# Spreading a two-way state-space scan between the q, k, v projections and the gate

## The chip, the cores and the metric

The kernel runs on one core of a Trainium2 chip. The metric is device time in microseconds of one execution, as the median of several runs. The engines of the core are TensorE (PE, with PEld for its weight loads), VectorE (DVE), ScalarE (ACT), GpSimd (POOL) and SyncE (SP); each works through its instructions in order, and they wait for each other through semaphores. SP and ACT also issue DMAs, each from its own in-order queue.

## The reference

One block of a hybrid encoder, 1024 tokens of 1024 channels in float32. The parts that the change touches are the state-space mixer and the q, k, v projections beside it:

```python
h = rmsnorm(x, norm_mix_w)
z, xbc, dt_raw, q, k, v = jnp.split(h @ w_in, offs, axis=-1)
# ssd_mixer, per direction, in chunks of 128 tokens, 16 heads of 64 in 2 groups, state 128:
a_cum = jnp.cumsum(ac, axis=2)
decay = jnp.exp(jnp.where(lower, a_cum[:, :, :, None] - a_cum[:, :, None, :], -jnp.inf))
cb = jnp.einsum("bclgn,bcsgn->bclsg", cc, bc)
y_diag = jnp.einsum("bclsge,bcsgep->bclgep", cb[..., None] * decay, xc)
chunk_states = jnp.einsum("bclgn,bclgep->bcgepn", bc, xc * decay_to_end[..., None])
_, h_in = lax.scan(lambda h, i: (i[1][..., None, None] * h + i[0], h), h0, (chunk_states, chunk_decay))
y_off = jnp.einsum("bclgn,bcgepn->bclgep", cc, h_in) * jnp.exp(a_cum)[..., None]
# y = forward + backward + d_skip * x, then
g = y * silu(z); g = g * rsqrt(mean(g * g) + eps) * norm_w     # per group of 512 channels
```

Behind it stand neighbourhood attention on q, k, v, an output projection over both halves, and a squared-ReLU MLP.

## The kernel before, in words

Every large product is made of three float32r matmuls: an operand is split into a rounded part (`hi`, a ScalarE copy) and a rest (`lo`, a subtraction on DVE or POOL), and `mm3` (L179-182) adds hi x hi, hi x lo and lo x hi in PSUM. A piece of a projection is 8 x 3 such matmuls, 128 rows by 512 columns.

The order of the program is: x, its norm and transposes; the convolution channels (px) and the decays; the gate z in 2 x 8 pieces (pz, SiLU into `zs` at L497, stored to sz_dr); then the scan together with the q, k, v projections; then attention with the output projection as filler; then the MLP. Weights of a projection come in four tiles of 512 KB (`wraw`, loaded on SP) that ScalarE and DVE split (`wh`, L150; `wl`, L151).

The scan and the projections are written one behind the other, and the framework's scheduler weaves them: it sets each engine's order from its own estimate of times. The scan is the loop over `i` and `g` that calls `backward(7 - i, g)` and `forward(i, g)`: 16 turns, in each a chunk of the backward and one of the forward direction. `backward` loads x (`xs`), multiplies C by B (`pcb`, L575), and makes the two-way decay block of eight heads in two halves: a 512 KB broadcast load of the running sums into `rb` (L593), two POOL subtractions (L600), a predicated copy on DVE that takes one direction below the diagonal and the other above (L606), the exponent on ScalarE (L611), the product with pcb on DVE (L613) and eight matmuls `pd` (L618; each is two halves in the trace). `carried` (py, L555) adds what the state of a direction brings into a chunk; `decay_state` (pS) moves the state on: it splits the weighed x (L528, L529), adds into `st` (L538) and splits the state (L541, L542). A partial sum of a chunk goes to y1_dr (the trace's y_dr) until the other direction comes by; `gated` (L562 to L567) multiplies with the gate, norms and stores to y_dr. pcb, py and pS share two PSUM buffers (`ps_s`).

`qkv_proj` makes 48 pieces (pq): q, k and v in eight pieces each, for each of two groups of heads, in three PSUM buffers. `normed_split` (L683 to L693 and the split after it) norms each q and k piece, transposes it (ptq) right behind it, splits it and stores it from the ScalarE queue.

The pools of the scan (`qs`) take the memory that the convolution's and gate's pool (`qp`) gave back, so the first scan tile waits for the last gate piece; the attention's pools take that of `qs`.

Of the kernel before, what the change touches and what calls it, by code (L numbers as in the profile page):

```python
# [56 lines left out]
def hymba_block(  # L57
# [66 lines left out]
    y1_dr = dr.tile([NT, P, D], F32, name="y1_dr")  # L124
# [54 lines left out]
    def mm3(pt, ah, al, bh, bl, first, last):  # L179
        nc.tensor.matmul(pt, lhsT=ah, rhs=bh, start=first, stop=False)  # L180
        nc.tensor.matmul(pt, lhsT=ah, rhs=bl, start=False, stop=False)  # L181
        return nc.tensor.matmul(pt, lhsT=al, rhs=bh, start=False, stop=last)  # L182

# [24 lines left out]
    with ExitStack() as ph:  # L208
# [21 lines left out]
        with ExitStack() as p0:  # L230
# [14 lines left out]
            for h in range(2):  # L245
# [31 lines left out]
                dg = rp.tile([P, 4, P], F32, tag="dg", name="dg")  # L277
# [29 lines left out]

        def proj_col(get, m, h, pt):
# [4 lines left out]

        with p1:
            qp = p1.enter_context(tc.tile_pool(name="qp", bufs=2, side="right", reuse_waits="tile"))
# [168 lines left out]


# [3 lines left out]
            for g in range(2):  # L489
                get = load_w_nat(w_in[0], 0, KD, OFF_Z + 512 * g, nc.vector)  # L490
                for t in range(NT):
                    pt = ps_mm("pz")
                    for k in range(KD):
                        s = (slice(None), k, slice(t * P, (t + 1) * P))
                        mm3(pt, hTh[s], hTl[s], *get(k), k == 0, k == KD - 1)
                    zs = qp.tile([P, 512], F32, tag="zs", name="zs")
                    nc.scalar.activation(zs, pt, AF.Silu, scale=rcol[:, t : t + 1])  # L497
                    nc.scalar.dma_start(szb[:, t, :, g * 512 : (g + 1) * 512], zs)

        def hb(v):  # L500
            return v.unsqueeze(2).broadcast_to([P, 8, HD])

        def h8(v):
            return v.rearrange("p (e d) -> p e d", d=HD)

        with ExitStack() as p2:
# [14 lines left out]
            st = [[None, None], [None, None]]  # L521

            def decay_state(d, c, g, xw):
                prev = st[d][g]
                pS = ps_s("pS")
                xh = qp.tile([P, 512], F32R, tag="xh", name="xh", bufs=1)
                xl = qp.tile([P, 512], F32R, tag="xl", name="xl", bufs=1)
                nc.scalar.activation(xh, xw, AF.Copy)  # L528
                nc.vector.tensor_tensor(xl, xw, xh.bitcast(F32), op=sub)  # L529
                mm3(pS, bNh[:, c, g, :], bNl[:, c, g, :], xh, xl, True, True)  # L530
                new = prev and prev[0]
                if prev is None:
                    new = qp.tile([P, 512], F32, tag=f"st{d}{g}", name="st", bufs=1)
                    nc.vector.tensor_copy(new, pS)
                else:
                    dec = ed[:, d, c, 8 * g : 8 * g + 8]
                    nc.gpsimd.tensor_tensor(h8(new), h8(new), hb(dec), op=mul)
                    nc.vector.tensor_tensor(new, new, pS, op=add)  # L538
# [182 lines left out]

# [680 lines left out]
```

## Time and profile before

| | us |
|---|---|
| median of 3 runs | 1671.18 (1670.56 to 1671.56) |
| the profiled execution | 1675.21 |
| its span, first to last instruction | 1673.4 |
| PE busy in the span | 1594.3 (95%) |
| DVE busy | 1027.3 (61%) |
| ACT busy | 722.5 (43%) |
| POOL busy | 721.8 (43%) |

A matmul's busy time runs until its end, and the next one starts before that, so a busy TensorE need not be at its pace: what counts is the time from start to start. The granted clock is 1.00 at full speed; a mean below that in a stretch means that part of it ran at half clock. A tile's number is left out in the names, so `y` is y1 and `c` is c1.

### The profile page before, as it was taken

Reading aid. Unit: us, or ns where it says so; the run is one execution under the profiler, and the core shown is the slowest. Engines: PE = TensorE matmul, PEld = TensorE weight load, DVE = VectorE, ACT = ScalarE, POOL = GpSimd, SP = SyncE. Lnnn points to the kernel's source line nnn. Section 1 sums busy time; section 2 is a strip of 40 time slices with the busy share of each in tenths; the row PEclk is TensorE's granted clock in tenths of the full one; section 3 lists DMA queues with packets and bytes.
Section 4 is the critical chain, followed back from the end, with each engine's and each line's share of the span. In section 5 each row is a group of like instructions: output and inputs, shape, how many; then the busy total and the mean of one; then the engine's idle time right before and its main releaser. Section 6 shows DMA issues by size and latency. Waiting matters only on the chain. (4 is left out here: it accounts for less than half of the span.)

```text
span 1673.4 us, 20880 instructions
## 1 busy us (share of the span) xinstructions
PE 1594.3 (95%) x7462; PEld 1296.9 (78%) x7462; DVE 1027.3 (61%) x1432; ACT 722.5 (43%) x1195; POOL 721.8 (43%) x520
## 2 busy tenths in 40 slices
PE   7999999899998899999999989999999979999999
PEld 6788888777776677887887777788888868888887
DVE  4777214889796852666675567434243388887863
ACT  5434223434343442566665433554444444433330
POOL 3000004788688762233334232344444465455551
PEclk9999999999999999999999999999999999999999
DMA  8113337776666884987674240343354386644331
GB/s 206 52 38 114 87 99 226 208 193 195 223 216 185 225 266 176 279 212 204 174 208 133 89 164 38 138 164 131 133 166 149 129 295 230 219 145 151 101 101 76
DMA packets 181026, 273.49 MB, mean 163 GB/s; under 512 B 14691, under 2 KB 105915, under 8 KB 180923
## 3 DMA queue, kind: packets, MB, share of 16 engines
q1 hardware_dynamic: 136939, 231.26, 45.3%
q10 hardware_dynamic: 42976, 37.23, 7.3%
q0 software_dynamic: 1008, 3.67, 0.5%
q8 instruction: 59, 0.97, 0.2%
q14 instruction: 44, 0.36, 0.1%
HBM read 188.88 MB, written 86.56 MB: 165 GB/s over the span
## 5 line engine op out<-in xcount | busy, mean ns | idle before, releaser
L748 POOL TENSOR_TENSOR wl<-wraw,wh 128x1024 fp32r<-128x1024 f32 x110 | 298.8, 2728 | 318.4 <-ACT wh L747 305.1
L747 ACT ACTIVATE wh<-wraw 128x1024 fp32r<-128x1024 f32 x110 | 115.5, 1054 | 151.3 <-PE px L733 51.3
L733 PE MATMUL px<-wh,ahl 128*128 128x512 f32 x512 | 160.9, 391 | 4.6 <-ACT ahl L747 3.3
L180 PE MATMUL pq<-wh,hTh 128*128 128x512 f32 x384 | 152.7, 400 | 4.8 <-ACT wh L150 4.8
L181 PE MATMUL pq<-wl,hTh 128*128 128x512 f32 x384 | 152.3, 398 | 5.2 <-DVE wl L151 5.2
L733 PE MATMUL px<-h,wh 128*128 128x512 f32 x496 | 155.8, 394 | 1.4 <-DVE x L1089 1.4
L182 PE MATMUL pq<-wh,hTl 128*128 128x512 f32 x384 | 152.0, 397 | 0.0
L748 DVE TENSOR_TENSOR ahl<-ar,ahl 128x1024 fp32r<-128x1024 f32 x56 | 114.8, 2058 | 23.2 <-ACT ahl L747 22.1
L747 ACT ACTIVATE ahl<-ar 128x1024 fp32r<-128x1024 f32 x56 | 58.2, 1052 | 140.0 <-PE px L733 76.3
L733 PEld LDWEIGHTS px<-wh,ahl 128*128 128x128 f32 x512 | 96.1, 188 | 26.0 <-ACT ahl L747 3.7
L733 PEld LDWEIGHTS px<-h,wh 128*128 128x128 f32 x496 | 92.8, 187 | 24.4 <-ACT h L186 1.6
L151 DVE TENSOR_TENSOR wl<-wraw,wh 128x1024 fp32r<-128x1024 f32 x40 | 54.7, 1373 | 82.5 <-ACT wh L150 81.9
L733 PE MATMUL px<-wl,ahl 128*128 128x512 f32 x256 | 99.9, 390 | 0.0
L733 PE MATMUL px<-h,wl 128*128 128x512 f32 x248 | 97.8, 394 | 0.0
L181 PEld LDWEIGHTS pq<-wl,hTh 128*128 128x128 f32 x384 | 72.9, 190 | 22.2 <-DVE wl L151 8.0
L180 PEld LDWEIGHTS pq<-wh,hTh 128*128 128x128 f32 x384 | 72.8, 190 | 21.5 <-ACT wh L150 7.1
L186 ACT ACTIVATE pth<-ptp 128x384 fp32r<-128x384 f32 (+1 forms) x128 | 56.8, 456 | 67.1 <-PE ptp L947 66.6
L600 POOL TENSOR_TENSOR rb<-rb,c 128x512 f32<-128x512 f32 x64 | 76.1, 1210 | 20.3 <-DMA rb<-cum_dr 17.4
L182 PEld LDWEIGHTS pq<-wh,hTl 128*128 128x128 f32 x384 | 72.9, 190 | 14.7
L150 ACT ACTIVATE wh<-wraw 128x1024 fp32r<-128x1024 f32 x58 | 61.0, 1057 | 53.1 <-PE px L181 24.1
L733 PE MATMUL pz<-h,wh 128*128 128x512 f32 x256 | 81.9, 400 | 0.7 <-DVE h L187 0.7
L733 PE MATMUL pz<-wh,ahl 128*128 128x512 f32 x256 | 80.5, 391 | 0.0
(271 smaller groups left out, 4081.2 us busy)
## 6 DMA issues: line engine op xcount, KB each, us to landing
ar<-act_dr SPq DMA_DIRECT2D x56, 512.0 KB, 3.6
act_dr<-cq SPq DMA_DIRECT2D x49, 512.0 KB, 3.0
wraw<-in_w_in_dram SPq DMA_DIRECT2D x44, 512.0 KB, 4.3
rb<-cum_dr SPq DMA_DIRECT2D x32, 512.0 KB, 6.7
wraw<-in_w_mlp_in_dram SPq DMA_DIRECT2D x32, 512.0 KB, 4.6
wraw<-in_w_mlp_out_dram SPq DMA_DIRECT2D x32, 512.0 KB, 4.2
q_dr<-hl ACTq DMA_DIRECT2D x64, 128.0 KB, 3.0
k_dr<-hl ACTq DMA_DIRECT2D x16, 512.0 KB, 4.4
```

The source lines that it names most:

```text
L150: nc.scalar.activation(hi[:, 0:n], raw[:, 0:n], AF.Copy)
L151: lo_eng.tensor_tensor(lo[:, 0:n], raw[:, 0:n], hi[:, 0:n].bitcast(F32), op=sub)
L180: nc.tensor.matmul(pt, lhsT=ah, rhs=bh, start=first, stop=False)
L181: nc.tensor.matmul(pt, lhsT=ah, rhs=bl, start=False, stop=False)
L182: return nc.tensor.matmul(pt, lhsT=al, rhs=bh, start=False, stop=last)
L186: top = nc.scalar.activation(hi, src, AF.Copy)
L600: nc.gpsimd.tensor_tensor(rb[:, d], rb[:, d], c1[:, d, c, h0 : h0 + 4].unsqueeze(2).broadcast_to([P, 4, P]), op=sub,)
L733: nc.tensor.matmul(pt, lhsT=a, rhs=b, start=f, stop=l, skip_group_check=True)
L747: nc.scalar.activation(hl[0], src, AF.Copy)
L748: eng.tensor_tensor(hl[1], src, hl[0].bitcast(F32), op=sub)
```

## The change

Nothing is computed otherwise; the order and the place of the scan's steps change.

- The backward states are made beside the gate (`beside`, called behind each of the 16 gate pieces and the first five q pieces): x is loaded at piece n, weighed and split at n + 2, multiplied at n + 4, and each state is stored to sb_dr for later.
- Twenty of the 32 half blocks of decays, before the exponent, are made there too, and stored to seg_dr; the other twelve in the scan's first steps. All these stores are issued on ScalarE, behind a piece's SiLU or square.
- The scan is 16 steps, group 0 first and then group 1, with chunks 0 to 7 in each; a step makes both directions of its chunk. `prepare` loads x, the finished blocks (`gm`), the backward state (`sb`) and takes the exponent; `carry`, `inside` and `carried` follow one piece of q, k, v, `carried` of the forward direction the next, and `finish` (pd, gate, store) the one after. `issue_after(mark)` keeps a step's matmuls behind the last matmul of that piece. Steps 1, 3, ... 13 have a further piece behind them.
- The transposes of a q or k piece stand behind the next piece.
- The sums y1_dr are gone, C is split once per chunk, and pcb takes its PSUM from the transposes' two buffers.

The diff, with the removed `decay_state`, `carried`, `backward`, `forward` and the two projection loops left out:

```diff
+        def normed(pt, rt):
+            qn = hp.tile([P, 512], F32, tag="qn", name="qn", bufs=2)
+            act = nc.scalar.activation(qn, pt, AF.Square, scale=rt)
...
+        def qkv_units():
+            held = None
+            for g in range(2):
+                for off in (OFF_Q, OFF_K, OFF_V):
+                    for b, pt, rt, mark in qkv_proj(off, g):
+                        if held is not None:
+                            held(mark)
+                            held = None
...
+                            qn, act = normed(pt, rt)
+                            held = partial(store_q if off == OFF_Q else store_k, g, b, qn)
+                        yield mark, act
...
+        def seg_make(rb, g, c, q):
+            h0 = 8 * g + 4 * q
+            for d in range(2):
+                nc.gpsimd.tensor_tensor(
+                    rb[:, d],
+                    rb[:, d],
+                    c1[:, d, c, h0 : h0 + 4].unsqueeze(2).broadcast_to([P, 4, P]),
+                    op=sub,
+                )
+            nc.vector.copy_predicated(
+                rb[:, 0], lmask.unsqueeze(1).broadcast_to([P, 4, P]), rb[:, 1]
+            )
+
+        def seg_store(rb, g, c, q):
+            nc.scalar.dma_start(seg_dr[g, c, :, q], rb[:, 0].rearrange("p h s -> p (h s)"))
...
+            pq.close()
+            zp = p1.enter_context(tc.tile_pool(name="zp", bufs=2, side="right", reuse_waits="tile"))
...
+            def beside(n, mark, act):
+                with tc.issue_after(act):
+                    while st_:
+                        c, g, new = st_.pop(0)
+                        nc.scalar.dma_start(sb_dr[g, c - 1], new)
+                    while made:
+                        seg_store(*made.pop(0))
+                if n - 4 in hl_:
+                    c, g = back[n - 4]
+                    hl = hl_.pop(n - 4)
+                    pS = ps_s("pS")
+                    with tc.issue_after(mark):
+                        mm3(pS, bNh[:, c, g, :], bNl[:, c, g, :], *hl, True, True)
...
+                if n - 2 in xs_:
+                    c, g = back[n - 2]
+                    hl_[n - 2] = weighed(zp, 3, 1, c, g, xs_.pop(n - 2))
+                for m in rb_.pop(n - 2, ()):
+                    made.append(m)
+                    seg_make(*m)
+                if n < 14:
+                    c, g = back[n]
+                    xs_[n] = zp.tile([P, 512], F32, tag="xs", name="xs", bufs=3)
+                    nc.sync.dma_start(xs_[n], xs_dr[c, :, g * 512 : (g + 1) * 512])
+                if 0 < n < 18:
+                    rb_[n] = []
+                    for _ in range(2 if n in (5, 9, 13) else 1):
+                        sg = segs.pop(0)
+                        rb_[n].append((seg_load(zp, 4, *sg), *sg))
...
+                    beside(8 * g + t, mark.ins, act.ins)
+            units = qkv_units()
+            for n in range(16, 21):
+                beside(n, *next(units))
...
+            for n, (c, g) in enumerate(steps):
+                xs, gms, chl, shl, xhl = held
+                if xhl:
+                    carry(c, g, xhl, mark)
+                y1 = inside(c, g, xs, gms)
+                if shl:
+                    carried(1, c, g, chl, shl, y1, mark)
+                while made:
+                    seg_store(*made.pop(0))
+                mark, _ = next(units)
                 if c > 0:
+                    carried(0, c, g, chl, ahead[g], y1, mark)
+                if xhl:
+                    ahead[g] = split_state(g)
+                if n + 1 < len(steps):
+                    held = prepare(*steps[n + 1])
+                if segs:
+                    sg = segs.pop(0)
+                    made.append((seg_load(qp, 1, *sg), *sg))
+                    seg_make(*made[-1])
+                mark, _ = next(units)
+                finish(c, g, xs, gms, y1, mark)
+                if n % 2 and n < 14:
+                    mark, _ = next(units)
+            for _ in units:
+                pass
```

How the order moves on TensorE. Before, in the middle of the q pieces (pq is a piece's product, pd the block's, pS and py the state's):

```order
L182 MATMUL pq<-wh,hTl 128x512
L618 MATMUL pd<-xs,rb 128x64 x4
L180 MATMUL pS<-xh,bNh 128x512
L181 MATMUL pS<-xl,bNh 128x512
L182 MATMUL pS<-xh,bNl 128x512
L618 MATMUL pd<-xs,rb 128x64 x4
L180 MATMUL py<-sh,ch 128x512
L181 MATMUL py<-sl,ch 128x512
L182 MATMUL py<-sh,cl 128x512
L693 MATMUL ptq<-ident,qn 128x128 x4
L180 MATMUL pq<-wh,hTh 128x512
```

After, among the v pieces, where one piece of 24 ends and the next begins (mm3 stands at L181 to L183 there):

```order
L183 MATMUL pq<-wh,hTl 128x512
L181 MATMUL pS<-xhl,bNh 128x512
L182 MATMUL pS<-xhl,bNh 128x512
L183 MATMUL pS<-xhl,bNl 128x512
L705 MATMUL pcb<-cT,bT 128x128
L181 MATMUL py<-shl,chl 128x512
L182 MATMUL py<-shl,chl 128x512
L183 MATMUL py<-shl,chl 128x512
L181 MATMUL pq<-wh,hTh 128x512
```

The block's product with pcb, its two halves and the state's steps stood together in one place; now pcb is one place and pd a later one, with two pieces, 48 matmuls, between them.

On ScalarE, at the end of the gate before (`zs` is SiLU of a gate piece, sz_dr its store, `wh` weight splits; then the scan begins):

```order
L150 ACTIVATE wh<-wraw 128x1024 x3
L497 ACTIVATE zs<-pz,rcol 128x512
L498 DMA sz_dr<-zs 16x8x512
L150 ACTIVATE wh<-wraw 128x1024
L550 ACTIVATE ch<-cT 128x128 x2
L528 ACTIVATE xh<-xw 128x512
L683 ACTIVATE qn<-pq,rcol 128x512 x2
```

And after, between two gate pieces (sb_dr takes a backward state, seg_dr a half block, xhl is a weighed x):

```order
L186 ACTIVATE xhl<-xw 128x512
L649 ACTIVATE zs<-pz,rcol 128x512
L604 DMA sb_dr<-st 128x512
L650 DMA sz_dr<-zs 16x8x512
L411 DMA seg_dr<-rb 128x512
L186 ACTIVATE xhl<-xw 128x512
```

Between two SiLUs there are now two more stores and a split, and each waits for what it stores or splits before the next SiLU can begin.

More of the change, by code (lines that the diff above doesn't have):

```diff
@@ L306, in hymba_block, with hb, h8, qkv_proj @@
         nc.sync.dma_start(dsk, d_skip.partition_broadcast(P)[:, 0, :])
+        def hb(v):
+            return v.unsqueeze(2).broadcast_to([P, 8, HD])
+        def h8(v):
+            return v.rearrange("p (e d) -> p e d", d=HD)
+        def qkv_proj(off, g):
+            get = load_w_nat(w_in[0], 0, KD, off + 512 * g, nc.vector)
+            for b in range(NT):
+                pt = ps_mm("pq")
+                for k in range(KD):
+                    s = (slice(None), k, slice(b * P, (b + 1) * P))
+                    mark = mm3(pt, hTh[s], hTl[s], *get(k), k == 0, k == KD - 1)
+                yield b, pt, rcol[:, b : b + 1], mark.ins
@@ new lines, in inside, with carried @@
+                y1 = qp.tile([P, 512], F32, tag="y1", name="y1")
+                nc.gpsimd.tensor_tensor(h8(y1), h8(xs), hb(cf), op=mul)
+                for gm in gms:
+                    nc.vector.tensor_tensor(
+                        gm, gm, cb.unsqueeze(1).broadcast_to([P, 4, P]), op=mul
+                    )
+                return y1
+            def carried(d, c, g, chl, hl, y1, mark):
+                py = ps_s("py")
+                with tc.issue_after(mark):
+                    mm3(py, *chl, *hl, True, True)
+                yo = qp.tile([P, 512], F32, tag="yo", name="yo")
+                e = e1[:, d, c, 8 * g : 8 * g + 8]
+                nc.vector.tensor_tensor(h8(yo), h8(py), hb(e), op=mul)
+                nc.gpsimd.tensor_tensor(y1, y1, yo, op=add)
@@ L665, in hymba_block @@
-            for i in range(NT):
-                for g in range(2):
-                    backward(NT - 1 - i, g)
-                    forward(i, g)
-            def qkv_proj(off, g):
-                get = load_w_nat(w_in[0], 0, KD, off + 512 * g, nc.vector)
-                for b in range(NT):
-                    pt = ps_mm("pq")
-                    for k in range(KD):
-                        s = (slice(None), k, slice(b * P, (b + 1) * P))
-                        mm3(pt, hTh[s], hTl[s], *get(k), k == 0, k == KD - 1)
-                    yield b, pt, rcol[:, b : b + 1]
@@ new lines, in finish @@
+                nc.vector.tensor_tensor(y1, y1, pd, op=add)
+                gated(y1, c, g)
+            steps = [(c, g) for g in range(2) for c in range(NT)]
+            held = prepare(*steps[0])
+            mark, _ = next(units)
+            ahead = {}
+            made = []
+            for n, (c, g) in enumerate(steps):
[8 more added lines that the diff above has]
+                mark, _ = next(units)
+                if c > 0:
+                    carried(0, c, g, chl, ahead[g], y1, mark)
[10 more added lines that the diff above has]
+                if n % 2 and n < 14:
+                    mark, _ = next(units)
```

268 lines of the change are left out of this document (114 added, 154 removed).

## Prediction

> **What bounds the kernel now.** I read the page, then the stretches (busy time by stage), then what TensorE waits for, then the order of its instructions in time. The time to beat is the profiled execution's, 1675.2 us with a span of 1673.4; it lies 4.0 above the median of the three runs, 1671.2, and I take what the sum saves off both alike. The stretches, from the gate to the start of attention; columns: busy us (and instructions) of PE, PEld, DVE, ACT, POOL, then granted clock, DMA share, GB/s:
>
> ```profile
> core 0: us, PE busy (x) PEld busy (x) DVE busy (x) ACT busy (x) POOL busy (x), PEclk, DMA share, GB/s
> 190.00:261.00 71.00, 71.00 (x315) 58.82 (x314) 7.39 (x7) 16.37 (x20) 0.00 (x0) 1.00 0.31 84
> 261.00:350.00 89.00, 82.79 (x401) 67.65 (x400) 63.35 (x95) 32.34 (x53) 61.53 (x56) 0.98 0.83 239
> 350.00:450.00 100.00, 89.74 (x429) 72.39 (x428) 87.16 (x127) 37.03 (x66) 81.95 (x71) 0.97 0.70 200
> 450.00:550.00 100.00, 88.07 (x407) 70.33 (x406) 80.09 (x112) 42.29 (x80) 81.98 (x78) 0.95 0.64 193
> 550.00:620.00 70.00, 64.33 (x309) 50.50 (x307) 48.52 (x70) 31.08 (x55) 49.98 (x54) 1.00 0.87 250
> 620.00:668.00 48.00, 45.46 (x206) 37.17 (x207) 14.49 (x19) 12.65 (x18) 10.82 (x11) 1.00 0.61 205
> ```
>
> The gate (first row) keeps TensorE full while DVE, POOL and the DMAs idle; the scan stage behind it crowds DVE and POOL to 80% and more and TensorE loses time. How much is lost takes the pace of each kind of matmul, since a busy time hides overlap. Two gate pieces of 24 matmuls end 5.44 us apart, so 0.227 a matmul; 16 pd halves take 1.70 us from start to start, four transposes 0.35:
>
> ```profile
> 195.95 0.69 ACT L497 ACTIVATE zs<-pz,rcol 128x512 f32<-128x512 f32 x1 [4.75 <-PE pz L182]
> 201.39 0.69 ACT L497 ACTIVATE zs<-pz,rcol 128x512 f32<-128x512 f32 x1 [4.75 <-PE pz L182]
> ...
> 337.93 1.89 PE L618 MATMUL pd<-xs,rb 128*128 128x64 f32 x16
> 339.63 0.48 PE L180 MATMUL py<-sh,ch 128*128 128x512 f32 x1
> ...
> 344.36 0.60 PE L693 MATMUL ptq<-ident,qn 128*128 128x128 f32 x4
> 344.71 0.48 PE L181 MATMUL pq<-wl,hTh 128*128 128x512 f32 x1
> ...
> L180 PE MATMUL pq<-wh,hTh x384: 386/390/775, 261.0 to 667.7; 128*128 128x512 f32 x192
> L182 PE MATMUL pq<-wh,hTl x384: 387/390/629, 261.7 to 668.1; 128*128 128x512 f32 x192
> ```
>
> The q, k, v pieces run from 261.0 to 668.1: 407 us. Their work at pace is 48 x 5.44 = 261.1, the scan's 168 wide matmuls 38.1, pd 16 x 1.70 = 27.2, pcb at pd's pace 3.4, transposes 32 x 0.35 = 11.2: 341. So 66 us are lost: 36.6 as idle time (the five rows' lengths less their PE busy), 9.8 to the clock (89 x 0.02 + 100 x 0.03 + 100 x 0.05), and 19.6 in stretched starts. What TensorE waits for there:
>
> ```profile
> PE pd L618 <- DVE rb L613: 7.3, 7, 2.3
> PE pcb L575 <- DVE yo L555: 6.6, 4, 2.5
> PE pq L181 <- DVE wl L151: 5.2, 7, 1.8
> PE pq L180 <- ACT wh L150: 4.8, 4, 2.1
> PE pd L618 <- issue: 3.0, 1, 3.0
> PE py L180 <- DVE yo L555: 2.3, 2, 1.7
> PE ptq L693 <- DVE qn L687: 2.0, 5, 1.0
> PE py L181 <- DVE sl L542: 1.7, 2, 1.2
> PE py L180 <- DVE st L538: 1.0, 1, 1.0
> ```
>
> Scan and transposes make 23.9 us of it (no one wait over 3.0), the weight splits at a change of piece 10.0.
>
> **The change part by part.** TensorE's work is the same, matmul for matmul; only its place moves. The engines do slightly less: twelve fewer splits of C. So everything turns on waits.
>
> Scan steps between pieces. The exponent product now stands one piece or more ahead of pd, and each carried matmul a full piece behind the state that it needs. A piece is 5.44 us, the longest listed wait 3.0: at today's lateness all 23.9 are covered. None would go if the lateness grew by as much as the cover. I take three quarters, 17.9, since the in-order queues of ACT and SP still couple the steps, and single buffers (split states, weighed x) still leave close pairs.
>
> The transposes a piece later are in that sum (the 2.0 row).
>
> Weight splits. Their order is unchanged; only DVE's load falls. The 20 blocks leave the stage with two POOL subtractions and one predicated copy each:
>
> ```profile
> L600 POOL TENSOR_TENSOR rb<-rb,c 128x512 f32<-128x512 f32 x64 | 76.1, 1210 | 20.3 <-DMA rb<-cum_dr 17.4 <-PE ptq L693 2.4 <-PE pq L182 0.3
> L606 DVE COPY_PREDICATED rb<-lmask,rb 128x512 f32<-128x512 int32 x32 | 40.6, 1268 | 15.9 <-POOL rb L600 15.8
> ```
>
> That is 20 x 2 x 1.21 = 48.4 us off POOL's 286 and 20 x 1.27 = 25.4 off DVE's 294 in the five stage rows, and the 14 backward states besides. In the gate, where DVE is idle, a change of weights costs TensorE nothing (71.00 of 71.00 busy). Between all and nothing I take half: 5.0.
>
> Clock. Four of the stage's five dips, each behind waits of 2 to 3 us that end at pd or pcb (the second behind two in a row), and the clock around two of them:
>
> ```profile
> 297.51 1.78 PE L618 MATMUL pd<-xs,rb 128*128 128x64 f32 x8 [3.03 <-issue]
> ...
> 353.24 1.10 PE L618 MATMUL pd<-xs,rb 128*128 128x64 f32 x8 [1.35 <-DVE rb L613]
> 355.19 0.47 PE L180 MATMUL pS<-xh,bNh 128*128 128x512 f32 x1 [0.84 <-ACT rb L611]
> ...
> 444.94 0.77 PE L575 MATMUL pcb<-cT,bT 128*128 128x128 f32 x2 [2.55 <-DVE yo L555]
> ...
> 525.16 2.59 PE L618 MATMUL pd<-xs,rb 128*128 128x64 f32 x16 [2.32 <-DVE rb L613]
> ...
> 290.00:303.00 13.00, 9.97 (x48) 8.32 (x47) 7.52 (x12) 4.83 (x8) 10.42 (x11) 0.87 0.86 260
> 438.00:448.00 10.00, 7.45 (x29) 5.80 (x28) 6.44 (x7) 2.45 (x5) 7.92 (x7) 0.83 0.60 164
> ```
>
> These are the waits that the new order covers, so the dips should go with them: between 0 and 9.8, and three quarters again, 7.4. The Trainium skill, page "TensorE: Matmul & The Clock Gate", section "HAM oscillation — how this bites in real kernels", puts the rule as no idle gaps above about 3.4 us. By it none of these gaps could have dipped the clock, the loss would have another source and stay, and the forecast would be 7.4 later.
>
> Stretched starts, 19.6: the same waits as the weight loads see them. Half, 9.8. Gains: 17.9 + 5.0 + 7.4 + 9.8 = 40.1.
>
> New costs. First, the gate's DMAs. From the order, in the 13 pieces from the first x load to the gate's end: 18 blocks in, 14 blocks out, 14 x loads, 11 state stores, 13 gate stores, 8 weight loads. Blocks in and weights are 512 KB, the rest 128x512 f32, 256 KB: 27.3 MB. The pieces last 13 x 5.44 + 36 x 0.227 = 78.9 us with the state matmuls, so 345 GB/s are wanted. The nearest rows, at the scan's start and in the fullest stretch:
>
> ```profile
> 260.00:280.00 20.00, 19.39 (x89) 15.71 (x87) 9.78 (x15) 7.89 (x12) 9.42 (x10) 1.00 0.94 286
> 610.00:630.00 20.00, 18.54 (x87) 14.76 (x86) 9.79 (x12) 6.85 (x9) 6.48 (x6) 1.00 1.12 348
> ...
> rb<-cum_dr SPq DMA_DIRECT2D x32, 512.0 KB, 6.7
> ```
>
> At 348 nothing is late; at 286/0.94 = 304 the gate ends 10.8 late. Who waits: SP holds x loads behind block loads that wait for a slot; ScalarE holds the next SiLU behind a block's store that waits for DVE; TensorE has three PSUM buffers before it notices, and the state matmul four pieces after its x load. I take 5. The Trainium skill, "DMA: Bandwidth & Descriptors", section "Specifications", gives about 358 GB/s of HBM per core. By that rule the gate just fits and the 5 fall away; the fullest row, 348, agrees.
>
> ScalarE also issues 25 new stores there; it is busy 16.4 of 71 us (first stage row), so issuing alone costs nothing. In the scan stage the traffic hardly changes: 32 loads of finished blocks, 14 of states and 18 block and 3 state stores of 256 KB come, 16.75 MB; 20 block loads and 28 transfers of partial sums, 17 MB, go; at a DMA share of 0.64 to 0.87 I cost that at nothing.
>
> Second, the scan's tiles take the gate helpers' memory, so its first loads wait for the last block's store. The order leaves three pieces (16.3 us) for store, load and split; 0 to 6, I take 2.
>
> Third, the entry to attention. The last scan step now has three pieces behind it instead of many, and attention's loads wait for the scan's memory. Today's loads take:
>
> ```profile
> 598.53 1.07 SPq L840 DMA_DIRECT2D q<-q_dr  x1
> ...
> 621.90 2.61 SPq L864 DMA_DIRECT2D braw<-t_dr  x1
> ...
> braw<-t_dr SPq DMA_DIRECT2D x16, 192.0 KB, 4.9
> ```
>
> From the first load to the bias landing: 621.9 + 2.6 + 4.9 - 598.5 = 30.9, and some 4 (estimate) of DVE, POOL and ACT before the first softmax transpose. TensorE has 16.3 of pieces and by the order some 12 of scores, transposes and output projection before it: 28. So 7 late, against 2.5 idle in the last stage row: 5 more, between -2.5 and 14. Costs: 12.
>
> Net 40.1 - 12 = 28.1: 1675.2 becomes 1647.1, the median 1671.2 becomes **1643**.
>
> **The rivals.** *Everything is covered* (0.13): no wait, stretch or dip is left but half the weights' 10, and costs halve: 61 - 6 = 55 saved, 1616; toward it speaks the wait-free gate. With part of that, 1622. *Half of it* (0.17): DVE and POOL still stand at 70% or so, the lateness follows the steps, and half the gains come: 20 - 12 = 8, 1663. *The clock loss stays* (0.05), since its source is not the gaps: 1643 + 7.4 = 1650; against it, every dip above has its gap. *The gate starves* (0.11): it decides below 27.3 MB in 78.9 + 33 us = 244 GB/s, where the lateness eats all. The scan stage moves 193 to 239 over long stretches with these same block loads; at the 200 of one of them the gate takes 136 us, 57 late, and the time is 1643 - 5 + 57 = 1695. Against it: those stretches wanted no more than that, and 286 was had with blocks in flight. *It changes nothing* (0.06): the waits come back as others of equal size, 1671; the order shows the moves done, so only size is open.
>
> **How the numbers follow.** The forecast case has 0.48, with 1630 to 1655 as its own range. 0.2% (3.3 us) is about what a measurement can tell from no change. Faster: forecast, full cover, kept clock and most of half, 0.48 + 0.13 + 0.05 + 0.15 = 0.81. Same: 0.06 + 0.02 = 0.08. Slower: 0.11. The range goes from 1620, into full cover, to 1673, past no change, and leaves out about half of full cover and the starved gate.
>
> **What would show it.** Right: the L618 and L575 waits all but gone from TensorE's list, granted clock 1.00 through the pieces, the stage shorter by 30, the DMA share near 1 in the gate with TensorE still full. Wrong: idle TensorE in the gate at the state matmuls (pS), long waits of ScalarE before SiLU there, or a hole of 10 us or more before the first softmax transposes.

## The result, and the profile after

The changed kernel takes 1657.1 us (median of 4 runs, 1654.3 to 1659.1) against 1671.4: a ratio of 0.9914 with an interval of 0.9897 to 0.9931, so 14.3 us faster. I had said 1643 with a range of 1620 to 1673. The profiled execution took 1659.05, its span 1657.3, 16.1 shorter than before.

The stretches of the changed kernel, cut at its own stages (the first row is the gate with blocks and backward states beside it; columns as in the prediction):

```profile
190.00:278.00 88.00, 83.59 (x350) 67.18 (x349) 44.90 (x43) 25.09 (x35) 58.82 (x53) 0.96 0.87 273
278.00:350.00 72.00, 65.39 (x301) 53.76 (x301) 41.75 (x58) 21.07 (x33) 37.73 (x37) 0.95 0.85 241
350.00:450.00 100.00, 93.41 (x466) 76.48 (x465) 73.38 (x116) 43.84 (x78) 68.56 (x67) 1.00 0.84 261
450.00:550.00 100.00, 91.25 (x447) 75.71 (x446) 68.53 (x103) 37.46 (x64) 60.01 (x56) 0.97 0.71 205
550.00:620.00 70.00, 70.00 (x360) 59.04 (x359) 51.16 (x85) 31.72 (x55) 41.23 (x40) 1.00 0.60 186
620.00:648.50 28.50, 28.50 (x136) 23.82 (x135) 6.50 (x11) 7.77 (x12) 8.49 (x10) 1.00 1.07 304
```

From 550 on TensorE is full, which it never was in the scan before. But the gate, full before, now idles for 4.4 us and is granted 0.96 of the clock, and there are losses until 550. What TensorE waits for in these stretches (us, times, longest):

```profile
PE pq L182 <- DVE wl L152: 6.7, 4, 4.9
PE ptq L342 <- DVE qn L334: 6.4, 3, 3.4
PE pq L181 <- ACT wh L151: 5.3, 3, 2.7
PE pz L181 <- ACT wh L151: 2.3, 1, 2.3
PE pz L182 <- DVE wl L152: 2.1, 2, 1.4
PE pq L181 <- DVE qn L334: 1.7, 1, 1.7
PE ptq L342 <- ACT gm L689: 1.6, 1, 1.6
```

The waits at pd, pcb and py are gone from the list. In their place stand the weight splits, `wl` and `wh`, with 16.4 us where they had 10.0, and the norms and transposes of q and k (the `qn` and `ptq` rows), with 9.7. Where time was won shows in the start times of the first of a piece's three matmuls (duration ns min/median/max, then first and last start):

```profile
L181 PE MATMUL pq<-wh,hTh x384: 387/389/774, 278.1 to 647.8; 128*128 128x512 f32 x192
...
L181 PE MATMUL pz<-wh,hTh x128: 387/389/628, 172.0 to 276.7; 128*128 128x512 f32 x128
```

From the first gate piece to the first q piece it takes 106.1 us. The work there is 87.0 for 16 pieces and 8.2 for the 36 state matmuls that now stand there, 95.2 at the prediction's pace: so measured, the gate ends 10.9 late (the kernel before, 1.8). The longest wait of TensorE, the 4.9 in the list, stands just behind this point, inside the first q piece. So the gate is better measured up to the second q piece, which begins at 290.9: that takes 118.9 us, where it took 94.3. Only the 8.2 of state matmuls are new work there, so 16.4 us are lost. From the first to the last q, k, v piece it takes 369.7, where it took 406.7. Behind that, attention up to the last output projection takes 352.2 (351.0 before), and the rest 656.9 (654.3 before).

What holds the weight splits can be read from VectorE's order in time. At the first q piece (GpSimd's subtraction, VectorE's copy and splits, then TensorE):

```profile
278.20 2.04 POOL L400 TENSOR_TENSOR rb<-rb,c 128x512 f32<-128x512 f32 x2 [1.48 <-DMA rb<-cum_dr]
280.27 1.55 DVE L406 COPY_PREDICATED rb<-lmask,rb 128x512 f32<-128x512 int32 x1 [2.37 <-POOL rb L400]
281.72 0.67 DVE L187 TENSOR_TENSOR xhl<-xw,xhl 128x512 fp32r<-128x512 f32 x1
282.32 4.33 DVE L152 TENSOR_TENSOR wl<-wraw,wh 128x1024 fp32r<-128x1024 f32 x3
283.58 0.79 PE L182 MATMUL pq<-wl,hTh 128*128 128x512 f32 x1 [4.90 <-DVE wl L152]
```

ScalarE had the first rounded weight at 274.5, but VectorE's queue is in order: the copy of a block waits for GpSimd, which waits for the block's load, and the splits stand behind it. The norms are held in the same way, through GpSimd, which has a step of theirs: the longest wait at a transpose ends at 493.63, and GpSimd's step (`rq`) could begin only at 490.26, behind the subtractions of a block whose load it had awaited for 10.64 us:

```profile
488.14 2.04 POOL L400 TENSOR_TENSOR rb<-rb,c 128x512 f32<-128x512 f32 x2 [10.64 <-DMA rb<-cum_dr]
493.63 1.09 PE L342 MATMUL ptq<-ident,qn 128*128 128x128 f32 x4 [3.37 <-DVE qn L334]
```

The groups of the subtractions and copies tell how much longer the blocks are waited for (busy us, mean ns, idle time before them and what ended it; before, 20.3 and 15.9 us of idle time stood here). A part of this idle time lies in the gate, where GpSimd and VectorE have little else to do, and is no harm in itself:

```profile
L400 POOL TENSOR_TENSOR rb<-rb,c 128x512 f32<-128x512 f32 x64 | 71.2, 1134 | 67.6 <-DMA rb<-cum_dr 57.0 <-DVE yo L732 4.4 <-DMA sz_dr<-zs 4.3
L406 DVE COPY_PREDICATED rb<-lmask,rb 128x512 f32<-128x512 int32 x32 | 39.6, 1239 | 54.2 <-POOL rb L400 49.2 <-DMA sz_dr<-zs 3.7 <-DMA wraw<-in_w_in_dram 1.3
```

### The profile page after: what moved, and what is told of

The parts are those of the page before. It is cut to its first block, busy times and chain, and to the rows that moved or that the text cites. A ratio compares the mean times of both kernels' runs of the same rounds, so it can differ in the third digit from the quotient of the medians.

```text
span 1657.3 us, 20925 instructions
## 1 busy us (share of the span) xinstructions
PE 1589.3 (96%) x7462; PEld 1300.0 (78%) x7462; DVE 1017.6 (61%) x1420; ACT 719.1 (43%) x1183; POOL 714.6 (43%) x520
## 5 line engine op out<-in xcount | busy, mean ns | idle before, releaser
L181 PE MATMUL pq<-wh,hTh 128*128 128x512 f32 x384 | 152.1, 401 | 7.0 <-ACT wh L151 5.3
L183 PE MATMUL pq<-wh,hTl 128*128 128x512 f32 x384 | 152.4, 398 | 0.0
L400 POOL TENSOR_TENSOR rb<-rb,c 128x512 f32<-128x512 f32 x64 | 71.2, 1134 | 67.6 <-DMA rb<-cum_dr 57.0
L181 PEld LDWEIGHTS pq<-wh,hTh 128*128 128x128 f32 x384 | 73.2, 191 | 22.8 <-ACT wh L151 6.6
L183 PEld LDWEIGHTS pq<-wh,hTl 128*128 128x128 f32 x384 | 73.3, 191 | 15.0
L181 PE MATMUL po<-wh,yh 128*128 128x512 f32 x192 | 76.5, 398 | 2.1 <-DVE x L888 1.8
```

The source lines that it names most:

```text
L400: nc.gpsimd.tensor_tensor(rb[:, d], rb[:, d], c1[:, d, c, h0 : h0 + 4].unsqueeze(2).broadcast_to([P, 4, P]), op=sub,)
```

## The experiments

Theory 1 is the reading above: an in-order queue that waits for a late block holds the splits. Theory 2 says that the DMAs are simply full in the gate. Theory 3 blames SyncE's queue, where weight loads stand behind block loads that wait for a buffer. All results first; the middle columns are from each kernel's profile (from the first gate piece to the first q piece, and to the second; from the first to the last q, k, v piece), and the last is the difference of the ratios times 1671.

| kernel | ratio to before, interval | gate | to the second q piece | q, k, v | against the change |
|---|---|---|---|---|---|
| before | 1 | 88.8 | 94.3 | 406.7 | +14.3 |
| the change | 0.9914 (0.9897 to 0.9931) | 106.1 | 118.9 | 369.7 | 0 |
| 1 no wait at the copy | 0.9926 (0.9906 to 0.9946) | 105.0 | 112.0 | 375.7 | +2.0 |
| 2 half blocks | 0.9874 (0.9856 to 0.9891) | 100.2 | 113.2 | 370.2 | -6.7 |
| 3 fourth raw weight | 0.9950 (0.9933 to 0.9967) | 104.4 | 117.1 | 377.1 | +6.0 |
| 4 blocks in the scan | 1.0010 (0.9998 to 1.0021) | 100.8 | 106.3 | 389.6 | +16.0 |
| 5 no wait at copy and store | 0.9865 (0.9844 to 0.9886) | 109.6 | 118.5 | 358.1 | -8.2 |
| 6 blocks worked on later | 0.9955 (0.9938 to 0.9972) | 104.0 | 119.0 | 378.6 | +6.9 |
| 7 stores on SyncE | 0.9891 (0.9873 to 0.9910) | 102.1 | 111.5 | 369.9 | -3.8 |
| 8 transposes at once | 0.9976 (0.9957 to 0.9994) | 104.3 | 119.4 | 378.9 | +10.4 |
| 9 a step later in the scan | 0.9854 (0.9836 to 0.9872) | 103.0 | 119.3 | 362.5 | -10.0 |
| 10 splits first in the gate | 0.9885 (0.9867 to 0.9902) | 104.9 | 110.4 | 366.6 | -4.8 |
| 11 both, exponents later | 0.9849 (0.9832 to 0.9866) | 105.0 | 110.5 | 361.9 | -10.9 |
| 12 and a fourth raw weight | 0.9861 (0.9841 to 0.9882) | 103.8 | 113.6 | 367.1 | -8.9 |

An interval is about 3 us to either side, so a difference below some 4 us in the last column is not told apart from none. The middle columns stand for one execution each. Experiments 8 and 9 leave the gate as it is: their first column still differs from the changed kernel's by 1.8 and 3.1, the second by no more than 0.5. So the gate is judged by the second.

**1. The copy waits for nobody.**

```diff
-                    op=sub,
+                    op=add,
...
-            nc.vector.copy_predicated(
-                rb[:, 0], lmask.unsqueeze(1).broadcast_to([P, 4, P]), rb[:, 1]
-            )
+            with tc.issue_after(phase["dv"].ins):
+                nc.vector.copy_predicated(
+                    scr[:, 0], lmask.unsqueeze(1).broadcast_to([P, 4, P]), scr[:, 1]
+                )
```

> VectorE makes its 32 predicated copies (the same size, in the same places of its queue) on a spare tile that nobody else uses, so that it no longer waits for GpSimd's subtractions; the selection is so left out of the result, and the subtractions are additions so that the exponents stay finite. Everything else, all transfers included, is as in the changed kernel. Theory 1 (VectorE's in-order queue: a copy that waits for a late block holds the weight splits and q norms behind it): TensorE's waits for wl and qn, 16.9 us in the changed kernel's pieces, and a part of the 7.6 us for wh go; 8 to 14 us faster than the changed kernel, so some 1643 to 1649 us, and the gate's last piece starts about 8 us sooner after its first. Theory 2 (the DMAs are full in the gate, whatever the order): within 2 us of the changed kernel, 1655 to 1659. Theory 3 (on SyncE's queue the fourth weight load stands behind block loads that wait for a buffer): 0 to 3 us faster.

No gain: theory 1, as it was put, is refuted. Up to the second q piece it is 6.9 us shorter, and behind that 11.7 longer. The profile shows a reason. What ScalarE waits for in the stretches from the gate on has a new row:

```profile
ACT hl L194 <- POOL rb L402: 21.2, 3, 7.8
```

The instruction in front of that `hl` on ScalarE is the block's store. With the copy out of the way the store waits for the subtraction, and ScalarE's half of the splits stands behind it. So the theory was widened to every in-order queue that waits for the block.

**2. Half the bytes per block.**

```diff
-                rb.rearrange("p d h s -> p d (h s)"),
-                cum_dr[:, r0 : r0 + 4, :].rearrange("d h s -> d (h s)").partition_broadcast(P),
+                rb[:, 0].rearrange("p h s -> p (h s)"),
+                cum_dr[0, r0 : r0 + 4, :].rearrange("h s -> (h s)").partition_broadcast(P),
```

> Each block load brings one direction's sums only, 256 KB instead of 512 KB; both additions (in place of the subtractions) read it, so instructions and their order of need stay, and the result is not the reference's. The gate's traffic falls by 20 x 256 KB = 5.2 of 27.3 MB. Theory 2 (the DMAs are full): the gate's lateness of about 16 us with the first q pieces goes for the most part: 8 to 14 us faster than the changed kernel. Theory 1 (VectorE's queue): a block lands some 2 to 3 us sooner, so GpSimd's and VectorE's waits shrink but stay: 3 to 6 us faster. Theory 3 (SyncE's queue): buffers come free a little sooner, 1 to 4 us faster.

6.7 us faster, between the two theories. Its place tells more: the gate is 5.9 shorter (5.7 up to the second q piece), and the q, k, v pieces are unchanged (370.2).

**3. A fourth raw weight buffer.**

```diff
-            phase["r"] += [wx]
+            phase["r"] += [wx] * 2
```

> A fourth buffer for raw weights in the projection phase, so that all four weight loads of a piece can be issued a whole group of pieces ahead and none waits for the first split of its own group; transfers are the same. Theory 1 (VectorE's queue): ScalarE's wait for late raw weights, 29.9 us in 7 waits, goes, but the splits themselves still stand behind the copies: 3 to 5 us faster than the changed kernel. Theory 2 (the DMAs are full): within 2 us. Theory 3 (SyncE's queue): 6 to 10 us faster, with the waits for wl after the change of weights gone too.

6 us slower than the changed kernel, which no theory gave. ScalarE's wait for raw weights left the head of its list, but the splits were late all the same. At the change of weights near 470 the whole chain can be read (GpSimd, VectorE, ScalarE's store and split, TensorE):

```profile
469.70 2.04 POOL L400 TENSOR_TENSOR rb<-rb,c 128x512 f32<-128x512 f32 x2 [5.73 <-DMA rb<-cum_dr]
471.77 0.73 DVE L406 COPY_PREDICATED rb<-lmask,rb 128x512 f32<-128x512 int32 x1 [7.05 <-POOL rb L400]
472.53 0.33 ACTq L411 DMA_DIRECT2D seg_dr<-rb  x1
473.54 1.06 ACT L151 ACTIVATE wh<-wraw 128x1024 fp32r<-128x1024 f32 x1 [8.94 <-DVE hl L195]
474.65 1.22 PE L181 MATMUL pq<-wh,hTh 128*128 128x512 f32 x2 [9.14 <-ACT wh L151]
```

The block's load had gone out at 463.6, when the block before it was stored, since the scan has one buffer for blocks. Its weights had long landed; TensorE idles 9.1 us for a block that it needs steps later.

**4. Most blocks made in the scan.**

```diff
-                if 0 < n < 18:
+                if n in (2, 5, 8, 11):
...
-                    for _ in range(2 if n in (5, 9, 13) else 1):
+                    for _ in range(1):
...
-                if segs:
+                for _ in range(min(2, len(segs))):
...
-                    made.append((seg_load(qp, 1, *sg), *sg))
+                    made.append((seg_load(qp, 2, *sg), *sg))
```

> Only 4 of the blocks are made beside the gate and the other 28 in the scan, two a step and two steps ahead; the backward states stay beside the gate and the scan stays split between the pieces. It tells what the 16 blocks beside the gate are worth. As I predicted (work moved from a crowded stage to an idle one): GpSimd gets 16 x 2 x 1.21 = 39 us and VectorE 16 x 1.27 = 20 us back in the scan, and 5 to 15 us of the gain are lost, 1662 to 1672 us. Theory 1: the gate's stalls at its change of weights (about 16 us up to the first q pieces) go, and come back as stalls of splits and norms in the scan, where the copies wait for blocks as before: within 4 us of the changed kernel. Theory 2: the gate gets its 16 us back and the scan, with 0.6 to 0.85 of the DMAs busy, loses less than that: 3 to 10 us faster.

The time of the kernel before: 16.0 us lost, about the whole gain and a little more than the 5 to 15 that I expected. By the profiles the 16 blocks beside the gate cost 12.6 up to the second q piece (118.9 against 106.3) and relieve what stands behind it by 27.2. But these blocks are worked on right behind their loads in the scan, which experiment 9 shows to be dear there; what they would cost in its order was not tried.

**5. Neither copy nor store waits.** As 1, and:

```diff
-            nc.scalar.dma_start(seg_dr[g, c, :, q], rb[:, 0].rearrange("p h s -> p (h s)"))
+            nc.scalar.dma_start(seg_dr[g, c, :, q], scr[:, 1].rearrange("p h s -> p (h s)"))
```

> As the first experiment, and the blocks' stores on ScalarE (same number, size and place) send a constant tile, so that they too wait for nothing; in the first experiment ScalarE's store waited for GpSimd's subtraction instead (its next instruction 21.2 us in 3 waits, up to 7.8). The blocks' values are so left out of the result; every transfer, every subtraction and copy is still made. Theory 1, widened (a block that lands late is waited for on an in-order queue, VectorE's by the copy and ScalarE's by the store, and the weight splits and norms stand behind it): 8 to 14 us faster than the changed kernel, 1643 to 1649 us on a chip where the kernel before takes 1671. Theory 2 (the DMAs are full: what TensorE waits for is the raw weights' own late landing): within 3 us of the changed kernel, since all bytes still move.

8.2 us faster, the lower end of the widened theory, with every transfer still made. TensorE's waits for splits are 9.7 us in all (16.4 in the changed kernel) and those for norms (`qn`) 5.2 (8.1). All of the gain lies behind the second q piece, 7.7 us there. Up to it nothing is won (118.5), although the first experiment, without one of the two waits, was 6.9 shorter there. Why is open.

**6. Blocks worked on later, still one buffer in the scan.** The copy beside the gate moves a piece later, and in the scan:

```diff
                     made.append((seg_load(qp, 1, *sg), *sg))
-                    seg_make(*made[-1])
                 mark, _ = next(units)
                 finish(c, g, xs, gms, y1, mark)
+                for m in made:
+                    seg_make(*m)
...
                 while made:
+                    seg_pick(*made[0])
                     seg_store(*made.pop(0))
```

> The whole computation, with each block worked on later after its load. Beside the gate the copy and the store come a piece later (three and four pieces after the load, with five buffers in place of four and one double load moved to the 15th piece); in the scan the subtractions stand behind the next piece and the step's pd, and copy and store in the next step. Theory 1, widened: VectorE's 49.2 us of waits for the subtractions fall below 20 and TensorE's waits for splits and norms to half: 5 to 10 us faster than the changed kernel, 1647 to 1652 us. Theory 2: within 3 us.

6.9 us slower, a miss. With one buffer a later store makes the next load later by as much. From 310 to 640 VectorE waits for subtractions more than in the changed kernel (21.4 in 6 waits), and the longest wait again has the splits behind it:

```profile
DVE rb L408 <- POOL rb L400: 25.8, 11, 7.3
```

**7. Stores on SyncE.**

```diff
-                        nc.scalar.dma_start(sb_dr[g, c - 1], new)
+                        nc.sync.dma_start(sb_dr[g, c - 1], new)
...
-            nc.scalar.dma_start(seg_dr[g, c, :, q], rb[:, 0].rearrange("p h s -> p (h s)"))
+            nc.sync.dma_start(seg_dr[g, c, :, q], rb[:, 0].rearrange("p h s -> p (h s)"))
```

> The blocks' and the backward states' stores go out from SyncE's queue instead of ScalarE's. Theory 1, widened: ScalarE no longer stands behind a late copy, but SyncE does, and the loads of weights, x and blocks behind it go out later by the same 5 to 9 us each time: 0 to 8 us slower than the changed kernel. Theory 2: no transfer is added or taken away, within 3 us.

Not slower, as theory 1 had it; 3.8 faster, with intervals that overlap, so a gain is not shown either. The profile's gate is 4.0 shorter, 7.4 up to the second q piece, and it moves more, not less:

```profile
190.00:278.00 88.00, 83.71 (x358) 67.84 (x356) 50.23 (x48) 25.09 (x35) 72.64 (x59) 0.98 0.94 299
```

So the 273 GB/s of the changed kernel's gate was no ceiling.

**8. Transposes at once.**

```diff
-                            held = partial(store_q if off == OFF_Q else store_k, g, b, qn)
+                            (store_q if off == OFF_Q else store_k)(g, b, qn, mark)
```

> The changed kernel with each q or k tile's transposes behind its own piece again instead of a piece later, as in the kernel before; nothing else is changed. By my prediction the transposes' waits were 2.0 us of the 23.9, so 1 to 4 us slower than the changed kernel. A rival: since the norm takes some 6 us of ScalarE, VectorE and GpSimd in turn, TensorE waits for it after each of the 32 pieces, and it is over 10 us slower.

10.4 us slower, with the rival's size but not by its mechanism. TensorE's list (from the gate to the end of these pieces) shows the wait at the transposes no longer than in the changed kernel (4.2 against 6.4 us for `qn`), and the splits later:

```profile
PE pq L182 <- DVE wl L152: 13.2, 7, 7.7
PE pq L181 <- ACT wh L151: 11.5, 2, 8.6
PE ptq L342 <- DVE qn L334: 4.2, 6, 1.2
```

Through which queue the earlier transposes delay the splits was not tried apart.

**9. Two buffers in the scan, and a step between load and work.** The subtractions and copy of a block, and its store, move to the step behind its load:

```diff
-                while made:
-                    seg_store(*made.pop(0))
+                for m in made:
+                    seg_make(*m)
                 mark, _ = next(units)
...
+                while made:
+                    seg_store(*made.pop(0))
...
-                    made.append((seg_load(qp, 1, *sg), *sg))
-                    seg_make(*made[-1])
+                    made.append((seg_load(qp, 2, *sg), *sg))
```

> The whole computation. In the scan each block has two buffers in place of one: it is loaded in one step and subtracted, copied and stored in the next, so that nobody waits for its load; the gate is left as it is. Theory 1, widened: the stalls in the scan at the changes of weights, where a block load waited for its only buffer, took some 6 us more to land and held VectorE and ScalarE (in the sixth experiment 7 to 9 us with the weight splits behind), go: 5 to 9 us faster than the changed kernel, a ratio to the kernel before of 0.986 to 0.989. Theory 2 (the raw weights' own late landing): within 3 us of the changed kernel, 0.990 to 0.993.

10.0 us faster than the changed kernel, a little more than theory 1 gave, 1647.6 in its own runs, and the whole computation is done. From 310 to 640, in the changed kernel VectorE waits for the subtractions, GpSimd for the blocks and SyncE for a buffer to be stored:

```profile
DVE rb L406 <- POOL rb L400: 21.4, 6, 6.8
...
POOL rb L400 <- DMA rb<-cum_dr: 33.2, 8, 10.6
...
SPq L391 <- DMA seg_dr<-rb: 39.7, 10, 8.6
```

and in this one:

```profile
DVE rb L406 <- POOL rb L400: 11.4, 7, 4.0
...
POOL rb L400 <- DMA rb<-cum_dr: 12.5, 7, 3.7
...
SPq L391 <- DMA seg_dr<-rb: 15.1, 6, 5.4
```

The stretch from 450 to 550, where the changed kernel had 91.25 of 100 us busy, is full:

```profile
450.00:550.00 100.00, 100.00 (x511) 84.63 (x510) 70.57 (x116) 46.42 (x81) 57.74 (x57) 1.00 0.66 203
```

There the changed kernel had lost 3.8 us in waits for splits, 4.9 in waits for norms and 3 to the clock. The traffic of the stretch is the same (205 and 203 GB/s), so the late block cost this time, and not the traffic. Elsewhere blocks still come late: TensorE waits 4.48 at 413.51 for a split that has a block's copy in front of it, and 8.11 at the first q piece. So its waits for splits add up to 18.8, no less than the changed kernel's 16.4. The second buffer alone was not tried; the later work without it is experiment 6.

**10. Splits first at the gate's changes of weights.** The next weights' loads and splits are written ahead of the blocks' work of the last piece, and the copies of four pieces queued behind the third split:

```diff
+                    if t == NT - 1:
+                        get = load_w_nat(w_in[0], 0, KD, (OFF_Z + 512, OFF_Q)[g], nc.vector)
                     beside(8 * g + t, mark.ins, act.ins)
...
                     made.append(m)
-                    seg_make(*m)
+                    if n % 8 in (0, 7):
+                        with tc.issue_after(splits[-2]):
+                            seg_make(*m)
+                    else:
+                        seg_make(*m)
```

> The whole computation. At the gate's two changes of weights the next weights' loads and splits stand ahead of the blocks' copies: the copies of the pieces 7, 8, 15 and 16 stand on VectorE behind the third of the four weight splits; the scan is left as it is. Theory 1, widened: the 4.9 us of waiting at the first q piece and a part of the 8 us at the gate's first change go: 4 to 9 us faster than the changed kernel, the gate's last piece begins about 100 us after its first instead of 105. Theory 2: the fourth weight lands as late as before, within 3 us.

4.8 us faster, inside what theory 1 gave, though its interval touches the changed kernel's. At the first q piece three splits now start at 275.94 instead of 282.32, and the 4.90 of TensorE's wait there are gone:

```profile
275.94 3.48 DVE L154 TENSOR_TENSOR wl<-wraw,wh 128x1024 fp32r<-128x1024 f32 x3
279.35 1.58 DVE L410 COPY_PREDICATED rb<-lmask,rb 128x512 f32<-128x512 int32 x1
```

The first column hardly shows it (104.9), since it ends in front of this wait. Up to the second q piece it is 110.4 us instead of 118.9, with the same transfers. In the second piece, at the fourth weight, TensorE waits 0.48 and 1.43 again, and up to the third it is 119.7 instead of 125.1.

**11. Both, and the exponents at their use.** 9 and 10 together, and `nc.scalar.activation(gm, gm, AF.Exp)` moved from `prepare` into the loop of `inside`.

> The whole computation: the ninth and the tenth together, and ScalarE's exponentials at the step that uses them instead of right behind their load, where they waited for it (16.3 us in 4 waits). Theory 1, widened: the gains add, 9 to 17 us faster than the changed kernel, a ratio of 0.981 to 0.986. Theory 2: within 4 us of the changed kernel, 0.989 to 0.994. A third way: with these waits gone the next one in line holds the splits, and it is no more than 5 us faster.

10.9 us faster, 1646.5 in its own runs: at the lower end of theory 1's range, and not to be told apart from the ninth alone. The gains don't add, as the third way had it, though its figure stood too low. Up to the second q piece 8.4 us are won, as in the tenth, but 1.9 of them are left up to the third (123.2): in the second piece TensorE waits 2.81 us for a weight split, until 287.17.

**12. And a fourth raw weight.** 11 with the edit of 3. In 11, on SyncE, the gate's fourth weight load stands behind a block load that waited for its buffer, and ScalarE waits for the weight:

```profile
223.98 0.37 SPq L395 DMA_DIRECT2D rb<-cum_dr  x1
224.44 0.43 SPq L152 DMA_DIRECT2D wraw<-in_w_in_dram  x1
...
231.97 1.06 ACT L153 ACTIVATE wh<-wraw 128x1024 fp32r<-128x1024 f32 x1 [10.62 <-DMA wraw<-in_w_in_dram]
```

> The whole computation: the eleventh with the fourth buffer for raw weights of the third. In the eleventh the fourth weight of the gate's second half still came late: its first split was done by 220.8, but its load went out at 224.4, right behind a block load that had waited for its buffer until 224.0, and ScalarE waited 10.6 us for it; at the first q piece 8.1 us. Theory 3 (SyncE's in-order queue, block loads ahead of the weight load), which the third experiment seemed to refute while VectorE still held the splits: those two waits go, TensorE's 4.2 and 2.8 us for wh with them and the half clock behind, 4 to 8 us faster than the eleventh, a ratio of 0.980 to 0.983. Rival: as in the third, no gain or a few us of loss (0.985 to 0.989), the splits being late for another reason.

No gain over the eleventh. The wait itself went: that split now starts at 222.18, and TensorE loses nothing there. Theory 3 is right about this one wait. Some 50 us later, though, VectorE stands behind a block again and TensorE behind VectorE, and up to the second q piece it takes 113.6 us against the eleventh's 110.5:

```profile
272.28 1.55 DVE L410 COPY_PREDICATED rb<-lmask,rb 128x512 f32<-128x512 int32 x1 [5.53 <-POOL rb L404]
...
274.54 0.47 PE L184 MATMUL pS<-xhl,bNh 128*128 128x512 f32 x1 [1.82 <-DVE st L621]
```

**What stays open: the gate.** Up to the second q piece 16.4 us are lost in the changed kernel. Splits ahead of the copies take 8.5 off, with the same transfers (10). Fewer blocks take 12.6 off (4), stores from SyncE 7.4 (7), smaller blocks 5.7 (2). So about half of the loss is the place of the splits behind the blocks, though a part of the gain goes again in the next piece. The rest, and what 11 and 12 lose again after each wait that they take away, speaks for the supply of blocks, by their bytes or by the turn of their four buffers; the runs don't separate these two. SyncE waits there for blocks to be stored before it can load the next (from 172 to 310 in the changed kernel):

```profile
SPq L391 <- DMA seg_dr<-rb: 54.5, 14, 7.2
```

## Why the prediction was right, and where it was not

The direction and the range held, but the range was 53 us wide; the size was half of what I forecast (14.3 of 28.1; 16.1 in the profiled execution). The measured time lies outside the 1630 to 1655 that I gave to the forecast case itself, and nearer to my rival of half the gains, 1663, than to the forecast. Of the signs that I named for being right, the waits at L618 and L575 went, but the clock, the stage's length and the full TensorE in the gate did not come. By the prediction's own sum, from the first gate piece to the last q, k, v piece: 496.0 became 476.3, against 428 of work at pace, so 68.0 lost became 48.3. Idle time went from 36.6 to 26.4, the clock's share from 9.8 to 10.1 (88 x 0.04 + 72 x 0.05 + 100 x 0.03), the rest, stretched starts, from 21.6 (1.9 of it in the gate) to 11.8. Against the forecast gains of 17.9, 5.0, 7.4 and 9.8 there came 16.6, -6.4, -0.3 and 9.8, in all 19.7.

- **Scan and transposes, 17.9 of 23.9: near in size.** pd, pcb and py are gone from the list. With three short rows that I had not listed (2.4) there were 26.3; 9.7 are left, all at norms and transposes, so 16.6 went. For the transposes themselves I was wrong: I held their waits to be covered, and they rose from 2.8 (2.0 of it in the 23.9) to 8.0, the longest behind a late block (at 493.63). Even so their delay is worth more than I gave it: undoing it costs 10.4 (experiment 8), through the splits.
- **Weight splits, 5.0: wrong, and this is the step that failed.** I wrote that their order is unchanged and that only VectorE's load falls. The load was not what mattered. The waits rose from 10.0 to 16.4, because blocks whose loads are late now stand ahead of the splits on VectorE and ScalarE. Experiment 5 shows it for the scan (9.7 without these waits), 9 for its stretch from 450 to 550, and 10 for the first q piece.
- **Clock, 7.4: wrong as a consequence.** The old dips went with their waits, as argued, and four came at the new waits where there had been five, with as much time in all.
- **Stretched starts, 9.8: came as forecast** (21.6 to 11.8). I had taken half without a reason for a half, and no run here tells what sets them, so that the figure fits is luck.
- **The gate, cost 5: too small, on a wrong ground.** That a change of weights costs TensorE nothing in the gate was true of a gate with nothing beside it. Its first row now loses 4.4 idle and 88 x 0.04 = 3.5 to the clock, 7.9, and up to the second q piece 16.4 are lost. The 10.8 that I worked out from a row at 286 GB/s, and then halved, looks like the 10.9 at the first q piece. I count that as luck: it took that row's rate for a ceiling, and experiment 7 moved 299 GB/s at a DMA share of 0.94. I had looked to TensorE at pS and to ScalarE at SiLU for signs; the sign was at wl and wh. The alternative by the Trainium skill ("DMA: Bandwidth & Descriptors", section "Specifications", some 358 GB/s), that the gate just fits and the 5 fall away, did not come: it moved 273.
- **The hand-off of memory, cost 2:** nothing; TensorE's list has no wait at the first scan step. **Entry to attention, cost 5:** 1.2 (351.0 to 352.2).
- **Not in my sum:** the part behind attention took 2.6 longer. It was left alone by the change, and over these profiles it lies between 652.0 and 656.9, so that is its scatter.

The measured sum is 19.7 - 1.2 - 2.6 + 0.2 (an earlier start) = 16.1.

## What to carry to other kernels

Work that is moved beside an idle stage is free only if nothing on the in-order queues ahead of that stage's own critical steps can wait for it: look at what stands in front of the weight splits on each queue, the issuing of a store included, and not at the engine's mean load. A block that is loaded, worked on and stored from one buffer can't be loaded ahead; a second buffer and a step between load and work gave 10 us here, and the step without the buffer lost 6.9. A wait that is removed can come back at the next late transfer, so judge it by the stage's length and not by the wait, and let the stage end behind the wait that you study: measured up to the first q piece, 8.5 us of gain in the tenth experiment can't be seen.

## What the runs showed of the hardware

The clock halves after shorter waits than one might think. In the changed kernel, two of its four dips in these stages (TensorE's waits before the first of them, then the granted clock around both):

```profile
226.56 0.50 PE L182 MATMUL pz<-wl,hTh 128*128 128x512 f32 x1 [1.41 <-DVE wl L152]
232.16 0.74 PE L181 MATMUL pz<-wh,hTh 128*128 128x512 f32 x2 [2.32 <-ACT wh L151]
```

```profile
222.00:233.70 11.70, 7.97 (x33) 5.66 (x31) 7.15 (x6) 1.58 (x2) 6.46 (x6) 1.00 0.89 296
233.70:240.50 6.80, 6.12 (x15) 4.70 (x15) 3.27 (x5) 1.32 (x2) 4.36 (x4) 0.50 0.74 231
276.00:281.50 5.50, 2.68 (x12) 1.87 (x10) 3.13 (x3) 1.75 (x2) 3.76 (x4) 1.00 0.72 210
281.50:288.30 6.80, 4.71 (x11) 3.75 (x12) 6.47 (x7) 0.79 (x1) 4.69 (x3) 0.50 0.88 272
```

One begins 2.8 us into a single wait, the 4.90 that ends at 283.58; the other follows waits of 1.41 and 2.32, whose ends lie 5.6 us apart. The Trainium skill, "TensorE: Matmul & The Clock Gate", section "HAM oscillation — how this bites in real kernels", asks for no idle gaps above about 3.4 us; here waits below that, close together, sufficed. Single waits of 1.70 and 2.22 us, which end at 347.41 and 415.84, had no dip behind them; in the kernel before, single waits of 2.55 and 3.03 had one (444.94 and 297.51, in the prediction).

The same predicated copy takes 0.72 us or 1.56. In the sixth experiment (VectorE, then what GpSimd did beside the first of the two; beside the second it was idle from 472.1 on):

```profile
460.01 1.56 DVE L408 COPY_PREDICATED rb<-lmask,rb 128x512 f32<-128x512 int32 x1 [1.94 <-POOL rb L400]
472.13 0.72 DVE L408 COPY_PREDICATED rb<-lmask,rb 128x512 f32<-128x512 int32 x1 [7.33 <-POOL rb L400]
...
459.94 1.04 POOL L724 TENSOR_TENSOR y<-xs,cf 128x512 f32<-128x512 f32 x1
```

The longer one began 0.07 us after a GpSimd instruction of 1.04 us, and is longer by 0.84. It is no single case. In the changed kernel 19 of the 32 copies began within a GpSimd instruction on a 128x512 tile that had 0.86 to 1.22 us left; each took that rest and 0.59 to 0.63 more. The other 13 began with none running, or 0.13 before its end, and took 0.73 to 0.76. The Trainium skill, "SBUF — State Buffer", section "SBUF: two separate sides", says that the two engines share a port pair which the first comer holds for its whole instruction; these rows agree. The mean of 1268 ns that I took for a copy from the profile before was thus a mean over both.
